# An encoder trunk in split fp32: when the reductions load their residual rows, and how the turns between stages are built

## The chip, the cores and the metric

The kernel runs on one core of one Trainium2 chip. The metric is the device time of one execution in microseconds (us), as the median of several runs; lower is better. The five engines run their own instruction streams in order: PE (TensorE, matrix products), DVE (VectorE), ACT (ScalarE), POOL (GpSimd) and SP (SyncE). In this kernel SP and POOL issue the DMAs, SP on the queue that the profile calls q1 and POOL on q0.

## What is computed

Two layers on a sequence of 1024 rows of 1024 floats. The even layer mixes with latent attention and a 2-D Fourier transform, the odd one with a spatial gating unit; each layer then has a SwiGLU block. Cut to what matters here:

```python
for layer in range(DEPTH):                       # 2
    y = even_mixer(x, ...) if layer % 2 == 0 else odd_mixer(x, ...)
    x = layer_norm(DN_ALPHA * x + y, mix_ln_g[layer], mix_ln_b[layer])
    x = layer_norm(DN_ALPHA * x + swiglu(x, ...), ffn_ln_g[layer], ffn_ln_b[layer])

def swiglu(x, w_gate, w_up, w_down):
    return (silu(x @ w_gate) * (x @ w_up)) @ w_down
```

So four times a matrix product with a wide inner dimension is followed by a sum with the residual rows x (times alpha) and a layer norm.

## The kernel before

Every product is made in split fp32: an operand is cast to a high part (ACT, line 135, names ending in h) and its remainder is formed as a low part (DVE, line 136, names ending in l). `mm3` (lines 141 to 143) then issues three matrix products per tile: high by high, low by high, high by low. The large products use Strassen's scheme in Winograd's form, seven block products of sums and differences of quarters instead of eight of the quarters.

The stages follow each other: the even mixer (0 to 566 us), `reduce` of its output, the first SwiGLU block, `reduce`, the spatial gating unit (`v_pair` and what follows), `reduce`, the second SwiGLU block, `reduce`.

`reduce` contracts a wide inner dimension (mix, ffn0, odd, ffn1 are its four calls). The inner dimension is cut into pages that earlier stages stored in memory, plain ones and sums of them (arrays named SA, SB, TA, TB). It runs the seven block products in the order p = 1, 5, 6, 4, 7, 2 and last 3, each over groups g of two pages. For each group `load` calls `stream`: SP loads the pages into tiles `rx` (pieces of 256 KB), ACT and DVE split them (tile `xoh`, `xol`), and PE multiplies them for four slots s. The call `load` runs a little ahead of the products. The residual rows are eight tiles `xt[half, s]` of 512 KB each, loaded by POOL in `residual` (line 450). Where the rows need the gain and offset of the layer norm before them, `gained` (lines 456 and 457, DVE) multiplies and adds. `add` (lines 444 and 446, DVE) adds a finished product, `norm` (lines 462 to 471) normalises, and `turn1`, `turn0` transpose the rows on PE into PSUM banks (line 363), take them back with gain and offset on ACT (line 365, one instruction per 128x128 block) and split them as operands of the next stage.

The slots of half 0 are turned at the start of the next stage, where `ffn` or `v_pair` calls the four closures in `turns`; `sums` (line 131 with splits) then forms the differences S2, S3, S4 of the turned operands. In `ffn` the unit u0 (`seven`) makes two products from the operands that are ready, u1 two more, and then the remaining ones of both. The weights of a unit are made into operands by `right_operands`: t4 and t1, b11 and b21, t2 and t3, b22. `behind` and `marks` tell the scheduler what a new instruction has to stand after; `marks[2]` is the low split of the latest load of the stream. The tiles x, q and y of `xt` are buffers which a store of the stage before may still be reading.

The order in which the instructions of each engine stand is the scheduler's, from the order of the code and these marks. On an engine nothing passes an instruction that waits.

## Time and profile before

| what | value |
|---|---|
| median of 3 runs | 2571.9 us (2570.29 to 2572.54) |
| the profiled execution, time and span | 2572.24 us, 2570.4 us |
| PE busy | 2471.8 us, 96% |
| DVE busy | 1840.0 us, 72% |
| ACT busy | 1073.5 us, 42% |
| POOL busy | 308.4 us, 12% |
| moved by DMA | 431.95 MB, mean 168 GB/s |

The span is the time from the first to the last instruction; the execution's own time is 1.8 us longer. Busy time of an engine is the time in which at least one of its instructions ran. PE's granted clock is given per stretch as a share: 1.00 is 2.4 GHz, 0.50 is 1.2 GHz. Times in the rows are us from the start of the span. In a timeline a bracket behind a row gives the time that the engine stood idle before it and what released it.

### The profile page before, as it was taken

To read this page: it belongs to the slowest core of one execution; us is meant where nothing else is said; L and a number is where in the kernel's file an instruction comes from. 1 tells how busy PE (TensorE), PEld (TensorE's weight loads), DVE (VectorE), ACT (ScalarE), POOL (GpSimd) and SP (SyncE) were. 2 spreads that over 40 slices of the span, in tenths; PEclk is the share of its full clock that TensorE was granted. 3 is DMA by queue.
4 is the path that set the end of the run, shared out by engine and by line. 5 is a ranking of instruction groups with operands and counts; after the bars stand their busy time and mean duration, and the time that the engine had idled before them with its cause. 6 is when DMAs were issued, how large, how long until landed. Compare 5 with 4: busy or idle time off the path is not lost. (4 is left out here: it accounts for less than half of the span.)

```text
span 2570.4 us, 33123 instructions
## 1 busy us (share of the span) xinstructions
PE 2471.8 (96%) x12294; PEld 2083.3 (81%) x12294; DVE 1840.0 (72%) x2673; ACT 1073.5 (42%) x1643; POOL 308.4 (12%) x511
## 2 busy tenths in 40 slices
PE   8989999999999999999999999898999999999997
PEld 6778888887778888878889997776878888887886
DVE  4448878757886667668677767788788766766757
ACT  3335545544653333334355442232474333333332
POOL 1000111010110111110011223221010101101001
PEclk9999999999999999999999999899999999999999
DMA  4122433147334454486645644457634544549554
GB/s 173 42 88 70 143 110 112 62 162 265 127 139 139 173 188 150 161 300 233 205 164 189 214 160 148 147 205 270 228 121 148 175 153 165 188 143 332 198 187 147
DMA packets 164073, 431.95 MB, mean 168 GB/s; under 512 B 19880, under 2 KB 26696, under 8 KB 163912
## 3 DMA queue, kind: packets, MB, share of 16 engines
q1 hardware_dynamic: 108216, 232.11, 27.5%
q0 software_dynamic: 55696, 197.73, 20.6%
q8 instruction: 96, 1.57, 0.3%
q14 instruction: 65, 0.53, 0.1%
HBM read 286.64 MB, written 138.41 MB: 165 GB/s over the span
## 5 line engine op out<-in xcount | busy, mean ns | idle before, releaser
L141 PE MATMUL b<-xoh,whi 128*128 128x512 f32 x1040 | 411.5, 396 | 20.3 <-ACT whi L135 18.4
L136 DVE TENSOR_TENSOR wlo<-raw,whi 128x1024 fp32r<-128x1024 f32 (+3 forms) x277 | 302.7, 1099 | 173.5 <-ACT whi L135 171.0
L135 ACT CAST whi<-raw 128x1024 fp32r<-128x1024 f32 (+3 forms) x277 | 260.6, 953 | 385.3 <-PE b L142 223.6
L135 ACT CAST xoh<-rx 128x1024 fp32r<-128x1024 f32 (+1 forms) x252 | 244.3, 1011 | 421.1 <-PE b L142 323.4
L143 PE MATMUL b<-xoh,wlo 128*128 128x512 f32 x1040 | 408.2, 393 | 0.3
L142 PE MATMUL b<-xol,whi 128*128 128x512 f32 x1040 | 408.3, 393 | 0.0
L136 DVE TENSOR_TENSOR xol<-rx,xoh 128x1024 fp32r<-128x1024 f32 (+1 forms) x252 | 287.3, 1168 | 166.1 <-ACT xoh L135 165.6
L142 PE MATMUL b<-xol,xoh 128*128 128x512 f32 x960 | 380.0, 396 | 17.7 <-DVE xol L136 17.7
L141 PE MATMUL b<-xoh 128*128 128x512 f32 x960 | 377.9, 396 | 14.5 <-ACT xoh L135 14.5
L143 PE MATMUL b<-xoh,xol 128*128 128x512 f32 x960 | 376.9, 393 | 0.0
L141 PEld LDWEIGHTS b<-xoh,whi 128*128 128x128 f32 x1040 | 197.7, 190 | 62.5 <-ACT whi L135 19.4
L143 PEld LDWEIGHTS b<-xoh,wlo 128*128 128x128 f32 x1040 | 197.1, 190 | 44.0 <-DVE wlo L136 3.1
L142 PEld LDWEIGHTS b<-xol,xoh 128*128 128x128 f32 x960 | 183.4, 191 | 59.1 <-DVE xol L136 21.0
L142 PEld LDWEIGHTS b<-xol,whi 128*128 128x128 f32 x1040 | 197.7, 190 | 41.0 <-issue 0.2
L141 PEld LDWEIGHTS b<-xoh 128*128 128x128 f32 x960 | 183.9, 192 | 54.2 <-ACT xoh L135 15.8
L143 PEld LDWEIGHTS b<-xoh,xol 128*128 128x128 f32 x960 | 183.0, 191 | 38.1
L624 ACT COPY y<-b 128x512 f32<-128x512 f32 x200 | 116.6, 587 | 214.2 <-PE b L143 210.1
L141 PE MATMUL b<-xah,whi 128*128 128x512 f32 x416 | 164.9, 396 | 0.1
L142 PE MATMUL b<-xal,whi 128*128 128x512 f32 x416 | 164.0, 394 | 0.0
L143 PE MATMUL b<-xah,wlo 128*128 128x512 f32 x416 | 162.4, 391 | 0.0
L131 DVE TENSOR_TENSOR raw<-raw,raw 128x512 f32<-128x512 f32 (+1 forms) x172 | 127.2, 739 | 24.0 <-DMA raw<-w_up 18.8
L669 DVE TENSOR_TENSOR y<-b,y 128x512 f32<-128x512 f32 x84 | 58.0, 690 | 81.4 <-PE b L143 81.4
(377 smaller groups left out, 4582.8 us busy)
## 6 DMA issues: line engine op xcount, KB each, us to landing
raw<-w_gate SPq DMA_DIRECT2D x44, 512.0 KB, 3.6
raw<-w_up SPq DMA_DIRECT2D x44, 512.0 KB
q<-w_down POOLq DMA_DIRECT2D x44, 512.0 KB, 5.2
h<-x POOLq DMA_DIRECT2D x44, 512.0 KB, 3.8
rx<-h SPq DMA_DIRECT2D x60, 256.0 KB, 3.1
rx<-w_down SPq DMA_DIRECT2D x60, 256.0 KB, 4.9
raw<-o_v SPq DMA_DIRECT2D x16, 512.0 KB, 5.2
x<-o_out POOLq DMA_DIRECT2D x16, 512.0 KB, 6.2
```

Of the source, the lines that this page charges most:

```text
L131: self.nc.vector.tensor_tensor(out, a, b, op=ALU.subtract)
L135: a = self.nc.scalar.copy(hi, src)
L136: return a.ins, self.nc.vector.tensor_tensor(lo, src, hi.bitcast(F32), op=ALU.subtract).ins
L141: mm(ps, lh, rh, start=start, stop=False, skip_group_check=skip)
L142: mm(ps, lh, rl, start=False, stop=False, skip_group_check=skip)
L143: mm(ps, ll, rh, start=False, stop=stop, skip_group_check=skip)
L624: nc.scalar.copy(t, ps)
L669: self.last_v = nc.vector.tensor_tensor(sb, ps, sb, op=op).ins
```

## The change

Four edits come together:

- `residual` takes one slot. Ahead of each load DVE writes one column of the tile (a memset of 128x1) that stands behind the low split of the latest load of the stream, and POOL's load comes after this memset. The loads of half 0 stand at groups 1 and 2 of product 1, those of half 1 in product 1's last group and product 5's first. Before, four loads stood together at group 1 of product 1 and four at group 0 of product 5.
- The first additions (product 1 into half 0) stand in group 1 of product 5 and not in the last group of product 1; the multiplications by gain and offset are spread one group later.
- `early_operands` makes the second unit's operands in two steps: t4 and t1 in the reduction, and the others behind `sums`.
- `turn0` takes two slots at once: 16 transposes into four banks, then 8 ACT instructions of 128x256 where there were 16 of 128x128, and one split of 128x1024 per operand. `ffn` turns two slots, runs two products of u0, turns the other two, and runs two of u1.

```diff
-        def residual(half):
-            for s in range(4):
-                nc.gpsimd.dma_start(xt[half, s], resid[token(half, s)])
+        def residual(half, s):
+
+            with self.behind(self.marks[2]):
+                nc.vector.memset(xt[half, s][:, 0:1], 0.0)
+            nc.gpsimd.dma_start(xt[half, s], resid[token(half, s)])
...
-                    residual(0)
                     last = self.job(st, M - 1, True) if st is self.stage["mix"] else None
-                if p == 5 and g == 0:
-                    residual(1)
+                if p == 1 and 0 < g < 3:
+                    for s in (2 * g - 2, 2 * g - 1):
+                        residual(0, s)
+                if (p == 1 and g == n - 1) or (p == 5 and g == 0):
+                    for s in (0, 1) if p == 1 else (2, 3):
+                        residual(1, s)
...
-                if p in (1, 5) and g > 1:
-                    spread([lambda s=s: gained(p == 5, s) for s in slots], g - 2, n - 2)
+                if p == 1 and g > 1:
+                    spread([lambda s=s: gained(0, s) for s in slots], g - 2, n - 1)
+                if p == 5 and g == 0:
+                    spread([lambda s=s: gained(0, s) for s in slots], n - 2, n - 1)
+                if p == 5 and g > 0:
+                    spread([lambda s=s: gained(1, s) for s in slots], g - 1, n - 1)
+                if (p, g) == (5, 1):
+                    for s in slots:
+                        add(0, s, lo, 1, True)
...
                     if g == n - 1:
-                        if p == 1:
-                            add(0, s, lo, p, True)
-                        elif p == 5:
+                        if p == 5:
...
+        def turn0(q):
+            ws = self.turned_two([xt[0, 2 * q + i] for i in range(2)], [self.m_tile("xq"[q]) for _ in range(2)], gT, bT)
+            for o, w in zip((self.A11, self.A12), ws):
+                self.late = self.split(*(x[:, q] for x in self.left(o)), w)[1]
+            for i in range(2):
+                kept[0, 2 * q + i] = tuple(w[:, :, i * P:(i + 1) * P] for w in ws)
...
+    def turned_two(self, zs, tiles, gT, bT):
+
+        nc = self.nc
+        ws = [t.rearrange("p (k c) -> p k c", k=4) for t in tiles]
+        pss = [self.bank(i, (P, 2, 256)) for i in range(4)]
+        for k in range(8):
+            for i, z in enumerate(zs):
+                nc.tensor.transpose(pss[k // 2][:, k % 2, i * P:(i + 1) * P], z[:, k * P:(k + 1) * P], self.ident)
+        for k in range(8):
+            nc.scalar.activation(ws[k // 4][:, k % 4, :], pss[k // 2][:, k % 2, :], AF.Identity, bias=bT[:, k:k + 1], scale=gT[:, k:k + 1])
+        return ws
...
+    def early_operands(self, w1, w2):
...
+        self.sub(v[:, hi], u[:, lo], g[:, lo])
+        self.sub(v[:, lo], u[:, hi], v[:, hi])
+        self.sub(v[:, lo], v[:, lo], g[:, hi])
+        cells(v, "t4", "t1")
+        yield out
+        cells(g, "b11", "b21")
+        self.sub(v[:, lo], u[:, hi], v[:, hi])
+        self.sub(v[:, hi], u[:, hi], u[:, lo])
+        cells(v, "t2", "t3")
+        cells(u[:, hi], "b22")
+        yield
...
-        u0 = unit(0, w0, "yq")
+        w1, rest = w1
+        u0, u1 = unit(0, w0, "yq"), unit(1, w1, "yq")
         turns[0]()
-        self.go(u0, 1)
+        self.go(u0, 2)
         turns[1]()
-        turns[2]()
-        self.go(u0, 1)
-        turns[3]()
-        u1 = unit(1, w1, "yq")
         self.go(u1, 2)
         sums()
+        next(rest)
         self.go(u0, 5)
...
-                if pend is not None and (n, b) in ((4, 0), (4, 1), (5, 0), (5, 1)):
-                    pend[0][(n - 4) * 2 + b]()
+                if pend is not None and b == 0 and n in (4, 5):
+                    pend[0][n - 4]()
```

What the change does to the order on the engines is shown at three places. In all rows the number behind L is the line in the kernel that the rows are of.

DVE in the reduction of ffn0, in product 1, before. L456 and L457 are the gain and offset on residual rows (`gb`), the tile x_9778 is the fourth one loaded, and the splits L136 of rx_9902 and rx_9907 are the operands of product 1's group 4.

```order
L316 TENSOR_TENSOR x_9759<-x_9573,x_9738 128x512
L317 TENSOR_TENSOR x_9758<-x_9573 128x512
L318 TENSOR_TENSOR x_9758<-x_9759,x_9573 128x512
L456 TENSOR_TENSOR q_9779<-q_9779,gb_9808 128x1024
L319 TENSOR_TENSOR x_9759<-x_9738,x_9758 128x512
L457 TENSOR_TENSOR q_9779<-q_9779,gb_9810 128x1024
L456 TENSOR_TENSOR x_9778<-x_9778,gb_9808 128x1024
L136 TENSOR_TENSOR xol<-rx_9902,xoh 128x1024
L457 TENSOR_TENSOR x_9778<-x_9778,gb_9810 128x1024
L136 TENSOR_TENSOR xol<-rx_9907,xoh 128x1024
```

The same place after. L464 is the memset, L471 and L472 are gain and offset; rx_9889 and rx_9894 are group 4, rx_9925 and rx_9930 group 5; x_9763 is the tile that was x_9778.

```order
L319 TENSOR_TENSOR x_9743<-x_9744,x_9558 128x512
L464 MEMSET x_9763 128x1
L136 TENSOR_TENSOR xol<-rx_9889,xoh 128x1024
L320 TENSOR_TENSOR x_9744<-x_9723,x_9743 128x512
L136 TENSOR_TENSOR xol<-rx_9894,xoh 128x1024
L471 TENSOR_TENSOR q_9764<-q_9764,gb_9793 128x1024
L472 TENSOR_TENSOR q_9764<-q_9764,gb_9795 128x1024
L136 TENSOR_TENSOR xol<-rx_9925,xoh 128x1024
L471 TENSOR_TENSOR x_9763<-x_9763,gb_9793 128x1024
L136 TENSOR_TENSOR xol<-rx_9930,xoh 128x1024
L472 TENSOR_TENSOR x_9763<-x_9763,gb_9795 128x1024
```

The multiplication of this tile stood ahead of both splits of group 4, and now stands between the two of group 5. Its load stood on POOL ahead of the stores ffn0SA and ffn0SB of the last page pair and now stands behind them.

POOL in the reduction of the odd mixer, before. L450 are residual loads, L814 stores a page (tp) which the stream loads again, L347 and L348 store sums of pages.

```order
L814 DMA tp_150<-x_14483 128x1024
L347 DMA oddSA_159<-raw_14829 128x1024
L348 DMA oddSB_167<-raw_14830 128x1024
L450 DMA x_14862<-xs_2_99 128x1024
L450 DMA x_14863<-xs_3_100 128x1024
L814 DMA tp_151<-x_14673 128x1024
L450 DMA q_14867<-xs_1_98 128x1024
L450 DMA q_14868<-xs_4_101 128x1024
L814 DMA tp_152<-x_14674 128x1024
```

The same place after, where L861 is the store of a page and L465 the residual load.

```order
L861 DMA tp_150<-x_14452 128x1024
L348 DMA oddSA_159<-raw_14798 128x1024
L349 DMA oddSB_167<-raw_14799 128x1024
L861 DMA tp_151<-x_14642 128x1024
L465 DMA x_14835<-xs_0_97 128x1024
L465 DMA y_14838<-xs_5_102 128x1024
L465 DMA q_14836<-xs_1_98 128x1024
L861 DMA tp_152<-x_14643 128x1024
L465 DMA q_14837<-xs_4_101 128x1024
```

The store of page tp_151 stood behind two residual loads and now stands ahead of all of them; tp_152 stands behind three.

ACT at the start of the first SwiGLU block, before. L365 takes a transposed block back from PSUM, whi_5994 is the high part of the second unit's t4 and t1.

```order
L365 ACTIVATE x_6664<-b_6665,bT_5615,gT_5614 128x128 x4
L365 ACTIVATE x_6664<-b_6666,bT_5615,gT_5614 128x128 x4
L135 CAST xah_6624<-x_6664 128x4x128 x2
L135 CAST whi_5996<-raw_5989 128x1024
L365 ACTIVATE q_6687<-b_6688,bT_5615,gT_5614 128x128
L624 COPY y_6662<-b_6649 128x512
L365 ACTIVATE q_6687<-b_6688,bT_5615,gT_5614 128x128 x3
L365 ACTIVATE q_6687<-b_6689,bT_5615,gT_5614 128x128 x4
L135 CAST xah_6624<-q_6687 128x4x128
L135 CAST whi_5994<-raw_5993 128x1024
```

The same place after, where L378 is the instruction for two slots; and, behind it, the place in the reduction of mix where the cast of t4 and t1 (now whi_6005) stands after.

```order
L378 ACTIVATE x_6622<-b_6625,bT_5615,gT_5614 128x256 x2
L378 ACTIVATE x_6622<-b_6626,bT_5615,gT_5614 128x256 x2
L135 CAST xah_6619<-x_6621 128x1024
L135 CAST xah_6619<-x_6622 128x1024
L135 CAST whi_6783<-raw_5997 128x1024
L378 ACTIVATE q_6684<-b_6686,bT_5615,gT_5614 128x256 x2
L378 ACTIVATE q_6684<-b_6687,bT_5615,gT_5614 128x256
L673 COPY y_6668<-b_6655 128x512
```

```order
L135 CAST xoh<-rx_6114 128x1024
L135 CAST xoh<-rx_6143 128x1024
L135 CAST whi_6005<-raw_6001 128x1024
L135 CAST xoh<-rx_6148 128x1024
L135 CAST xoh<-rx_6177 128x1024
```

The cast of t4 and t1 has left the turn for the reduction, and 16 instructions of 128x128 for a pair of slots have become 8 of 128x256.

## Rows read from the trace of the kernel before

**Rows 1.** PE's waits over the span: who waited for whom, total us, times, longest.

```profile
PE b L141 <- ACT whi L135: 18.4, 5, 6.0
PE b L142 <- DVE xol L136: 17.7, 8, 5.4
PE b L141 <- ACT xoh L135: 14.5, 3, 7.0
...
PE b L862 <- DVE y L873: 2.9, 2, 2.1
```

**Rows 2.** Busy us by engine (count), granted clock, DMA share, GB/s, by stretch.

```profile
1135.00:1160.00 25.00, 19.61 (x81) 15.81 (x80) 20.41 (x23) 6.40 (x7) 3.62 (x7) 0.93 1.02 385
1363.00:1400.00 37.00, 32.57 (x247) 31.72 (x247) 36.82 (x64) 20.91 (x33) 11.23 (x21) 0.93 0.66 226
```

**Rows 3.** The same view, two stretches behind PE's first stop in mix's reduction.

```profile
571.80:578.50 6.70, 6.16 (x14) 4.49 (x15) 2.41 (x2) 1.12 (x2) 0.00 (x0) 0.51 1.04 400
578.50:585.00 6.50, 6.50 (x30) 5.34 (x29) 5.50 (x8) 4.13 (x4) 0.00 (x0) 0.98 0.90 332
```

**Rows 4.** Timelines of POOL, PE and SP, reduction of mix: start, us, engine, line.

```profile
558.69 1.05 POOL L450 DMA_DIRECT2D q<-x  x2 [8.41 <-PE mm L143]
...
571.78 0.72 PE L141 MATMUL b<-xoh 128*128 128x512 f32 x1 [2.37 <-ACT xoh L135]
...
588.09 0.54 POOL L340 DMA_DIRECT2D mixSB<-raw  x1 [1.20 <-DVE raw L319]
...
594.09 0.32 SPq L383 DMA_DIRECT2D rx<-mixSB  x1
...
598.12 0.80 PE L141 MATMUL b<-xoh 128*128 128x512 f32 x1 [5.14 <-ACT xoh L135]
```

**Rows 5.** Timelines of ACT and PE, start of the first SwiGLU block.

```profile
705.87 1.20 ACT L135 CAST whi<-raw 128x1024 fp32r<-128x1024 f32 x1
...
707.12 0.80 PE L141 MATMUL b<-xoh,whi 128*128 128x512 f32 x1 [5.00 <-ACT whi L135]
...
724.09 0.62 ACT L135 CAST xoh<-q 128x512 fp32r<-128x512 f32 x1 [1.45 <-DVE q L131]
...
727.13 0.50 PE L141 MATMUL b<-xoh,whi 128*128 128x512 f32 x1 [0.97 <-ACT q L624]
```

**Rows 6.** Groups of ACT's instructions, 695 to 730: busy us, mean ns, idle before.

```profile
L365 ACT ACTIVATE q<-b,bT,gT 128x128 f32<-128x128 f32 x16 | 6.3, 609 | 0.0
...
L624 ACT COPY y<-b 128x512 f32<-128x512 f32 x4 | 2.5, 646 | 0.0
```

**Rows 7.** Timelines of POOL, DVE and PE, reductions of ffn0 and ffn1.

```profile
1139.61 0.53 POOL L450 DMA_DIRECT2D x<-xs  x1
...
1144.51 1.22 DVE L456 TENSOR_TENSOR x<-x,gb 128x1024 f32<-128x1024 f32 x1 [4.59 <-DMA x<-xs]
...
1149.20 0.80 PE L142 MATMUL b<-xol,xoh 128*128 128x512 f32 x1 [5.39 <-DVE xol L136]
...
2361.15 0.79 PE L142 MATMUL b<-xol,xoh 128*128 128x512 f32 x1 [4.94 <-DVE xol L136]
```

**Rows 8.** DMA issues, 1139.6 to 1140: KB each, us from issue to landing.

```profile
x<-xs POOLq DMA_DIRECT2D x1, 512.0 KB, 9.4
```

**Rows 9.** Timelines of POOL, ACT and PE, reduction of the odd mixer.

```profile
1743.62 0.53 POOL L450 DMA_DIRECT2D x<-xs  x1 [6.05 <-DMA tp<-x]
1744.15 0.54 POOL L814 DMA_DIRECT2D tp<-x  x1
...
1758.01 0.79 PE L141 MATMUL b<-xoh 128*128 128x512 f32 x1 [7.02 <-ACT xoh L135]
...
1770.12 0.80 PE L142 MATMUL b<-xol,xoh 128*128 128x512 f32 x1 [3.05 <-DVE xol L136]
```

**Rows 10.** DMA issues, 1744.1 to 1744.6: KB each, us to landing.

```profile
tp<-x POOLq DMA_DIRECT2D x1, 512.0 KB, 7.9
```

**Rows 11.** One line's instructions: DVE's smallest form, ns min, median, max, first and last start.

```profile
L205 DVE TENSOR_SCALAR rs<-mv x32: 135/146/155, 659.0 to 2561.2; 128x1 f32<-128x1 f32 x32
```

More of the change, by code (lines that the diff above doesn't have):

```diff
@@ L488, in turn1 @@
             kept[1, s] = l, h
-        def turn0(s):
-            l, h = self.turned(xt[0, s], (0, 1) if s % 2 == 0 else (2, 3), self.m_tile("xxqq"[s]), gT, bT)
-            self.split(*self.operand(self.A11, s), l)
-            self.late = self.split(*self.operand(self.A12, s), h)[1]
-            kept[0, s] = l, h
+        def turn0(q):
[4 more added lines that the diff above has]
+                kept[0, 2 * q + i] = tuple(w[:, :, i * P:(i + 1) * P] for w in ws)
         def sums(s):
@@ L579, in all_sums @@
                     sums(s)
-        return [lambda s=s: turn0(s) for s in slots], all_sums
+        return [lambda q=q: turn0(q) for q in range(2)], all_sums
     def bcast(self, t, src):
```

15 lines of the change are left out of this document (13 added, 2 removed).

## The prediction

> **What bounds the kernel now.** The table first: PE is busy for 96% of the span, so nothing that DVE, ACT or a queue saves counts unless PE stands still for it. PE's waits over the whole span come next [rows 1]. Three causes make up most of it: the high split of weights (18.4 us), the low split of stream operands (17.7 us) and their high split (14.5 us), 50.6 us together, plus 2.9 us for a DVE subtraction of the spatial unit. They come in a few long stops, 5 to 7 us at most, and not in many short ones. The timelines then say where the stops are: in the reduction of mix 2.37 and 5.14 us [rows 4], at the start of the first SwiGLU block 5.00 and 0.97 us [rows 5], in the reductions of ffn0 and ffn1 5.39 and 4.94 us [rows 7], in the reduction of the odd mixer 7.02 and 3.05 us [rows 9]. The second SwiGLU block starts like the first.
>
> A stop costs more than its length. Behind the first one in mix, PE ran 14 matmuls in 6.7 us with a granted clock of 0.51 (1.2 GHz), and after that 30 in 6.5 us at 0.98 (2.4 GHz) [rows 3]. At the later pace of 0.217 us the 14 would take 3.0 us. So that stop cost another 3.6 us. For other stops I take half of it, 1.8 us, between 0 and 3.6.
>
> **The change part by part.** I go by places, since in a reduction two of the four edits act together.
>
> *Reduction of mix.* Before, POOL issues its eight residual loads from 558.69 on [rows 4], the moment the stream is starved: over 571.8 to 578.5 the DMA engines are full, share 1.04 at 400 GB/s [rows 3], and PE waits for an operand until 571.78. After, no residual load is issued before the low split of the latest stream load has run, so the 2.37 us go and with them the 3.6 us of slow clock, 6.0 us. PE is then ready for the second stop at 593.0 - 6.0 = 587.0 (its start of 598.12 less 5.14 is 593.0). That stop is a store followed by its own load: POOL issues mixSB at 588.09, SP may load it at 594.09, when it has landed, and PE starts 4.0 us later [rows 4]. In the new order the eight residual loads, 4.2 MB, stand ahead of that store on POOL's queue. If they start at about 567 and have between all and half of the 400 GB/s, they take 10.5 to 21 us, and are done between 578 and 588; the store can then land between 585 (when its sums, formed late in product 1, are ready) and 592, and PE starts at 589 to 596 instead of 598.1. The gain of the whole place is 2 to 9 us; I take 5.5, the middle.
>
> The Trainium skill speaks against this edit: "DMA: Bandwidth & Descriptors", section "Rules for kernel authors", advises to issue a DMA early, compute, and wait for its semaphore late, so that the fixed cost is overlapped. By that rule the residual rows, needed only at the first additions, stood well where they were, and the edit gains nothing here; rows 3 speak the other way, since what is early there takes bytes from something that is needed sooner.
>
> *Reductions of ffn0 and ffn1.* The stop at 1149.20 ends with the low split of group 4. DVE had stood for 4.59 us in front of it, at a multiplication by the gain whose residual tile landed at 1144.5 [rows 7]. The order of the change puts both splits of group 4 ahead of any multiplication. This removes 5.39 and 4.94 us and 1.8 us each for the clock, 13.9 us together. Next late is the same tile's multiplication, now between the splits of group 5. Its load stands behind two stores and not ahead of them, like the load that POOL issues at 1139.61 and that lands 9.4 us later [rows 8], at 1149.0. Without the stop PE wants group 5 at 1149.2 - 5.4 + 5.3 (24 matmuls at 0.22) = 1149.1. Split and multiplication take 1.22 us each, so if the tile lands at 1149.0, group 5's second split ends at 1151.4, and PE stops for up to 2.3 us, plus up to 1.8 us for the clock; with one residual load less ahead of it, it lands earlier and the stop goes. I subtract 1.5 us per reduction: 11 us for both, between 6 and 14.
>
> *Reduction of the odd mixer.* POOL stands for 6.05 us in front of a residual load until 1743.62, since an old store still reads the tile. Behind it waits the store of page tp, issued at 1744.15 [rows 9] and landed 7.9 us later [rows 10], at 1752.1; PE starts 5.9 us after that, at 1758.01. In the new order this store has no residual load ahead of it. If it is issued 2 us earlier and moves without the two loads (1 MB, 2.6 us at 400 GB/s), it lands 4.6 us earlier. The second stop, 3.05 us before 1770.12, comes from a split behind the first additions, which wait for the end of product 1; these now stand a group later, and the stop goes with 1.8 us of clock. Together 9.5 us, and up to 14 if all of both stops goes. Against it: a memset or a multiplication that waits for a late tile can take the additions' place, as in the other reductions; at worst nothing is gained. I take 7.5, between 0 and 14.
>
> *Starts of the two SwiGLU blocks.* PE waits until 707.12 for the high split of the second unit's t4 and t1, which ACT makes at 705.87 [rows 5]; the change makes it in the reduction. The 5.00 us stop and the slow clock behind it (1.8 to 3.6 us) go, so PE does the four products without a break and is through at 726.2 - 5.0 - 2.7 = 718.5, where it stopped at 726.2 before. But the fifth needs operands of `sums`, and that chain runs on ACT and DVE: ACT still casts for it at 724.09, and the low part on DVE comes after that. What makes the chain start earlier is the turning by twos: 16 instructions of 128x128 took 6.3 us, 0.39 each, and a copy of 128x512 takes 0.62 (4 in 2.5 us) [rows 6]; a third of the way between them, 128x256 takes about 0.47 and 8 take 3.8. That is 2.5 us of ACT per pair and 5.0 per turn at most. From this the chain's end moves from 725.4 (724.09 + 0.62 + 0.69 of DVE) to some 722, between 720.5 and 725.4. PE then waits from 718.5, a stop of 2 to 7 us at a new place with slow clock behind it, and resumes 2 to 6.6 us before 727.13, of which the clock takes up to 2.7 us. The net is -1 to 6.6 us per block. I take 1.5 each, 3 us, nearer to the lower end, because DVE's part of the chain is no shorter.
>
> *Start of the spatial unit.* DVE is busy 36.82 of 37 us there [rows 2], and PE waits 2.9 us for its subtractions [rows 1]. DVE's work is the same, but its chain may start as much earlier as ACT finishes the turns, up to 2.5 us per pair, and a low split of weights stands earlier in its order. I take 3 us, between 0 and 7 (the 2.9, the short stops beside it, and a clock of 0.93 over 37 us, worth 2.6).
>
> *What is added.* 32 memsets of one column; DVE's smallest form in this trace takes 0.146 us [rows 11], so 4.7 us, 1.2 per reduction. DVE is busy 20.41 of 25 us in such a stretch [rows 2], and the memsets lie in its idle time: 0, and 4.7 us if all of them fall in front of a split that PE waits for. PE's transposes are as many as before.
>
> The sum is 5.5 + 11 + 7.5 + 3 + 3 = 30 us. From the profiled execution, 2572.2 us, that leaves 2542.2; it stands 0.3 us above the median, so I forecast 2542 us.
>
> **The rivals.** *Slower: DVE waits for the later residual rows.* On DVE nothing passes an instruction that waits. The loads of half 1 are now tied to splits in the last group of product 1 and the first of product 5, and their multiplications begin in group 1 of product 5. Two groups of PE are 10.6 us; a load took 9.4 us [rows 8]. If a load takes longer than these two groups, each multiplication stands in front of a split of the stream. One such stop is worth 5.4 + 1.8 = 7.2 us (what rows 7 show for the same wait); two in each of the three reductions with gain are 43 us, against the 30 gained: 2572 + 13 = 2585 us. For it: 9.4 is near to 10.6, and the DMA engines are full there (share 1.02 [rows 2]). Against: half of the loads are gone from the stretch just before.
>
> *Same: the bytes only move.* In 1135 to 1160 the DMA engines are at their limit, 385 GB/s [rows 2]. If it is the sum of stream and residual bytes that sets the pace of products 1 and 5, what one group gains the next loses, and only the two starts bring something: about 2569 us, between 2565 and 2573. The Trainium skill's rule on early issue ("DMA: Bandwidth & Descriptors", "Rules for kernel authors") would give the same. Against it: the stops end with single late pieces, and between them PE does not wait.
>
> *Half: the chains of store and load stay.* The stores of mixSB and tp remain late behind residual loads on POOL's queue, the starts of the blocks swap one stop for another with nothing left. Then mix gives 2, odd 3, ffn 9, the spatial unit 0: 2558 us.
>
> *More: all stops named go.* These are 2.4 + 5.1 + 2 x 6 + 5.4 + 4.9 + 7.0 + 3.1 + 2.9 = 42.8 us, and some 1.8 us or more for each of nine; about 60 us, 2512 us.
>
> **How the numbers follow.** My forecast has a chance of 0.45, and covers 2530 to 2553. Half 0.20, more 0.11, same 0.12, slower 0.12. Some 0.2% (5 us) is what a measurement of this kernel can tell from no change. Faster by over that is 0.45 + 0.20 + 0.11 and a little of the same case, 0.78; same 0.11; slower 0.11. The range that leaves out no more than 2 in 10 goes from 2517 (most of the case of more) to 2566 (all of the half case); left out are the slower case and most of the same one.
>
> **What would show it.** Right: no stop of PE over 1 us at the places of 571.8, 707.1, 1149.2, 1770.1 and 2361.2; the load of mixSB issued before 592; tp landed before 1749; the stop of the SwiGLU starts moved to the first product that uses `sums`. Wrong: a wait of DVE at the multiplication by the gain in front of a split of product 5, a memset that waits for a store, or a stop in front of group 5 longer than 2.3 us.

## The result and the profile after

| | before | after |
|---|---|---|
| median | 2572.2 us (4 runs, 2570.3 to 2576.7) | 2552.4 us (4 runs, 2550.5 to 2552.7) |
| ratio to before | | 0.9925, interval 0.9911 to 0.9938 |
| profiled execution, time and span | 2572.24, 2570.4 us | 2552.27, 2550.5 us |
| PE busy | 2471.8 us | 2465.7 us |
| DVE busy | 1840.0 us | 1840.6 us |
| ACT busy | 1073.5 us | 1062.7 us |

The change is faster by 19.9 us, 0.75%, clear of the interval. The forecast was 2542 us, 30 us faster; the time lies in the range 2517 to 2566. A third of the gain forecast did not come. The runs below say which terms were off, and the largest error lies in one of them.

The same view as in [rows 1], PE's waits of the kernel after, has these rows (who waited for whom, total us, times, longest):

```profile
PE b L141 <- ACT xoh L135: 19.8, 6, 6.0
PE b L142 <- DVE xol L136: 13.1, 9, 3.9
PE b L141 <- ACT whi L135: 8.9, 3, 6.4
```

Half of the wait for the high split of weights is gone, and a quarter of the wait for low splits. The row of the high splits `xoh` has grown, but not by the stream: 7.9 of its 19.8 us are two stops for the operands that `sums` makes, 3.72 and 4.18 us at the starts of the SwiGLU blocks, so one wait has taken another's place there. For operands of the stream it fell from 14.5 to 11.9 us.

**Where the time went.** PE runs 12,294 matmuls and transposes in both traces. The start of the one with a given number can be compared between two traces, so the difference at the end of a stage less that at its beginning is what the stage gained. This table has it in us (negative is earlier), for the change and for all runs of this study, each against the kernel before. The stages are, by the times of before: mix 566 to 640, start of the first SwiGLU block 693 to 760, ffn0 1118 to 1260, start of the spatial unit 1345 to 1440, odd 1745 to 1800, start of the second SwiGLU block 1893 to 1945, ffn1 2330 to 2400. "Rest" is all else.

| kernel | mix | start 1 | ffn0 | spatial | odd | start 2 | ffn1 | rest | sum |
|---|---|---|---|---|---|---|---|---|---|
| forecast | -5.5 | -1.5 | -5.5 | -3.0 | -7.5 | -1.5 | -5.5 | 0 | -30.0 |
| after | -5.1 | -1.8 | -4.4 | -6.5 | +1.5 | -0.1 | -5.0 | +1.4 | -20.0 |
| e1 tie only | -3.5 | +0.3 | -2.5 | -0.3 | -3.9 | +0.2 | -4.3 | -1.6 | -15.6 |
| e2 additions only | -0.1 | +0.1 | -3.0 | -0.2 | +1.9 | +0.7 | -3.7 | -1.0 | -5.3 |
| e3 early operands only | +1.0 | +1.3 | +1.2 | -1.1 | -0.3 | +4.1 | -0.1 | -1.2 | +4.9 |
| e4 turns by twos only | +0.2 | -0.2 | -0.3 | -6.5 | -0.3 | +0.2 | +0.2 | +0.2 | -6.5 |
| e5 after, odd's places undone | -3.3 | -2.7 | -4.2 | -6.5 | -0.5 | -0.8 | -5.0 | +0.3 | -22.7 |
| e6 after, no early operands | -3.4 | -0.4 | -4.2 | -6.5 | +1.6 | +0.6 | -4.1 | -3.2 | -19.6 |
| e7 after, no memset | -0.5 | -2.9 | -2.7 | -6.2 | +2.1 | -0.4 | -5.9 | -0.9 | -17.4 |
| e8 e5 and sums by operand | -3.9 | -7.3 | -4.0 | -6.3 | -0.8 | -5.7 | -5.0 | -2.4 | -35.4 |
| e9 e8, mix later, order | -1.0 | -7.2 | -7.1 | -6.2 | -1.2 | -5.7 | -8.1 | +0.2 | -36.3 |
| e10 e8, odd's loads last | -3.5 | -7.2 | -4.0 | -6.0 | +1.1 | -5.7 | -4.9 | -1.3 | -31.5 |
| e11 e9, behind the load | -3.4 | -7.2 | -7.1 | -6.3 | -1.5 | -5.7 | -8.1 | +0.2 | -39.1 |
| e12 e8 and order | -3.6 | -7.2 | -7.1 | -6.3 | -0.8 | -5.7 | -8.1 | -3.2 | -42.0 |

"Rest" moves by 3 us and more between kernels whose code there is the same, and a stage by 1 to 2; the last section shows why. So only differences above some 2 us in one stage are read as an effect of an edit, unless the stops behind them are named.

**The places, in the profile of after.** Mix, timelines of POOL, PE and SP, as in [rows 4]:

```profile
569.13 0.54 POOL L465 DMA_DIRECT2D x<-x  x1 [4.04 <-DVE x L464]
...
580.26 0.54 POOL L341 DMA_DIRECT2D mixSB<-raw  x1 [0.66 <-DVE raw L320]
...
590.28 0.50 PE L141 MATMUL b<-xoh 128*128 128x512 f32 x1 [3.78 <-ACT xoh L135]
...
593.39 0.32 SPq L396 DMA_DIRECT2D rx<-mixSB  x1
...
599.85 0.50 PE L141 MATMUL b<-xoh 128*128 128x512 f32 x1 [1.14 <-ACT xoh L135]
```

The residual loads wait for the memset and start at 569.13, where seven of the eight started from 558.69 on and one at 549.75. The first stop of [rows 4] is gone. The store of mixSB is issued 7.8 us earlier than before and its load only 0.7 us earlier, so it landed 12.5 us after its issue and not 6.0. The DMA issues from 580.2 to 580.7 (KB, us to landing) say so:

```profile
mixSB<-raw POOLq DMA_DIRECT2D x1, 512.0 KB, 12.5
```

The reduction of ffn0, timelines of DVE and PE, as in [rows 7]:

```profile
1141.87 1.23 DVE L471 TENSOR_TENSOR x<-x,gb 128x1024 f32<-128x1024 f32 x1 [5.06 <-DMA x<-xs]
1143.01 1.22 DVE L136 TENSOR_TENSOR xol<-rx,xoh 128x1024 fp32r<-128x1024 f32 x1
...
1144.28 0.50 PE L142 MATMUL b<-xol,xoh 128*128 128x512 f32 x1 [1.18 <-DVE xol L136]
...
1153.60 0.50 PE L142 MATMUL b<-xol,xoh 128*128 128x512 f32 x1 [0.86 <-DVE xol L136]
```

DVE still stands for 5 us in front of the same late tile, but now between the splits of group 5, and PE pays 1.18 us for it where it paid 5.39, with no slow clock behind it.

The reduction of the odd mixer, timelines of POOL, PE and DVE, as in [rows 9]:

```profile
1723.65 0.60 POOL L861 DMA_DIRECT2D tp<-x  x1 [5.18 <-DVE wlo L846]
...
1738.41 0.79 PE L141 MATMUL b<-xoh 128*128 128x512 f32 x1 [6.01 <-ACT xoh L135]
...
1759.68 1.19 PE L141 MATMUL b<-xoh 128*128 128x512 f32 x4 [0.96 <-ACT xoh L135]
...
1762.97 2.37 DVE L471 TENSOR_TENSOR x<-x,gb 128x1024 f32<-128x1024 f32 x2
1765.24 2.36 DVE L472 TENSOR_TENSOR x<-x,gb 128x1024 f32<-128x1024 f32 x2
1767.52 1.29 DVE L457 SCALAR_TENSOR_TENSOR x<-x,b 128x512 f32<-128x512 f32 x2
...
1772.30 6.91 DVE L136 TENSOR_TENSOR xol<-rx,xoh 128x1024 fp32r<-128x1024 f32 x6
...
1774.72 0.50 PE L142 MATMUL b<-xol,xoh 128*128 128x512 f32 x1 [3.86 <-DVE xol L136]
```

The store of tp took 6.5 us to land, by the DMA issues from 1723.6 to 1724:

```profile
tp<-x POOLq DMA_DIRECT2D x1, 512.0 KB, 6.5
```

The first stop is 6.01 us where it was 7.02. The second one (3.05 us at the end of product 1) is gone, and two new ones stand in product 5 and at the start of product 6: the last multiplications and eight additions stand ahead of the split that PE waits for. The view by stretch (PE, PEld, DVE, ACT, POOL busy, clock, DMA share, GB/s) shows DVE without a pause from 1750 to 1774:

```profile
1738.00:1750.00 12.00, 11.59 (x39) 9.34 (x40) 11.61 (x13) 4.27 (x5) 2.63 (x5) 0.73 0.75 260
1750.00:1762.00 12.00, 11.04 (x49) 8.84 (x48) 12.00 (x14) 4.11 (x4) 0.00 (x0) 1.00 0.76 272
1762.00:1774.00 12.00, 8.86 (x40) 7.00 (x38) 12.00 (x15) 4.00 (x4) 0.00 (x0) 1.00 0.29 92
```

The starts of the two SwiGLU blocks, PE's stops, as in [rows 5]:

```profile
718.24 1.89 PE L141 MATMUL b<-xoh,whi 128*128 128x512 f32 x3 [3.72 <-ACT xoh L135]
...
1919.46 1.89 PE L141 MATMUL b<-xoh,whi 128*128 128x512 f32 x3 [4.18 <-ACT xoh L135]
```

The stop for the weights' split is gone and stands in front of the first product that uses `sums`, as forecast.

### The profile page after: what moved, and what is told of

It is laid out like the page before. It is cut to its first block, busy times and chain, and to the rows that moved or that the text cites. A ratio compares the mean times of both kernels' runs of the same rounds, so it can differ in the third digit from the quotient of the medians.

```text
span 2550.5 us, 33081 instructions
## 1 busy us (share of the span) xinstructions
PE 2465.7 (97%) x12294; PEld 2077.1 (81%) x12294; DVE 1840.6 (72%) x2695; ACT 1062.7 (42%) x1583; POOL 309.5 (12%) x511
## 4 chain that ended last, share of the span: by engine, by line
PE 76%; DVE 9%; issue 6%; DMA 4%; ACT 3%; SPq 1%; POOL 1%; DVEq 0%; ACTq 0%; POOLq 0%
PE b L142 17%; PE b L143 17%; PE b L141 17%; PE S L1313 6%; PE b L909 5%; PE mm L141 4%; PE mm L142 4%; PE mm L143 4%; PE mm L1332 2%; DVE xol L136 2%; DMA rx<-h 1%; ACT xoh L135 1%; DVE raw L131 1%; SPq L396 0%; DMA oddSA<-raw 0%
## 5 line engine op out<-in xcount | busy, mean ns | idle before, releaser
L136 DVE TENSOR_TENSOR wlo<-raw,whi 128x1024 fp32r<-128x1024 f32 (+3 forms) x277 | 302.4, 1099 | 163.3 <-ACT whi L135 161.9
L136 DVE TENSOR_TENSOR xol<-rx,xoh 128x1024 fp32r<-128x1024 f32 (+1 forms) x252 | 287.7, 1168 | 141.2 <-ACT xoh L135 130.6
L141 PE MATMUL b<-xoh 128*128 128x512 f32 x960 | 373.6, 394 | 11.9 <-ACT xoh L135 11.9
```

The costliest lines, as they stand in the source:

```text
L136: return a.ins, self.nc.vector.tensor_tensor(lo, src, hi.bitcast(F32), op=ALU.subtract).ins
L141: mm(ps, lh, rh, start=start, stop=False, skip_group_check=skip)
```

## The experiments

Each kernel was run beside the kernel before on the same chip. The median of the kernel before was 2568.6 to 2572.2 us in the five groups of runs (after; e1 to e4; e5 to e8; e9 and e10; e11 and e12), so across groups the ratios are compared. The numbers by stage are those of the table above, each from one trace.

**e1, the tie alone.** In the kernel before, `residual` and the places of its calls as in the change, all else as before.

```diff
-        def residual(half):
-            for s in range(4):
-                nc.gpsimd.dma_start(xt[half, s], resid[token(half, s)])
+        def residual(half, s):
+            with self.behind(self.marks[2]):
+                nc.vector.memset(xt[half, s][:, 0:1], 0.0)
+            nc.gpsimd.dma_start(xt[half, s], resid[token(half, s)])
...
+                if p == 1 and 0 < g < 3:
+                    for s in (2 * g - 2, 2 * g - 1):
+                        residual(0, s)
```

> The kernel before with one edit: residual loads one slot at a time behind a memset, in the new places; multiplications, first additions, operands and turns as before. Theory (the tie lets the stream's loads go first, the shift of the multiplications is what removes the stops in the reductions of ffn0 and ffn1): mix gains about 5 us, the odd reduction 0 to 4, ffn0 and ffn1 lose or gain under 2 each, since the multiplication of a late tile still stands ahead of group 4's splits and its tile lands later; in total 2563 to 2568. Rival (the tie alone makes the gain of all reductions): 2554 to 2558. Rival (the bytes only move): 2570 to 2574.

Measured: 2556.5 us (2553.6 to 2556.9), ratio 0.9938 (0.9923 to 0.9952), inside the range of the first rival. The loads in their new places and tied bring most of the whole change alone, though some 3 of its trace's 15.6 us are clock (see the last section). What the new places bring in the kernel before without the tie was not run; e7 has that with the other edits. My theory is wrong on ffn0 and ffn1: they gain 2.5 and 4.3 us without any shift of the multiplications in the code. The tie changes DVE's order too. These rows are the two splits of group 4 and the multiplication of the late tile in ffn0:

```profile
1136.55 2.35 DVE L136 TENSOR_TENSOR xol<-rx,xoh 128x1024 fp32r<-128x1024 f32 x2
...
1144.97 1.23 DVE L458 TENSOR_TENSOR x<-x,gb 128x1024 f32<-128x1024 f32 x1 [2.53 <-DMA x<-xs]
```

The multiplication now stands behind both splits, as in the change, and PE stops at group 5, for 2.66 us where it was 5.39.

**e2, the shift of multiplications and additions alone.** In the kernel before, `gained` one group later and the first additions at product 5's second group.

```diff
+                if p == 5 and g > 0:
+                    spread([lambda s=s: gained(1, s) for s in slots], g - 1, n - 1)
+                if (p, g) == (5, 1):
+                    for s in slots:
+                        add(0, s, lo, 1, True)
```

> The kernel before with one edit: multiplications one group later and the first additions in product 5's second group; residual loads as before. Theory: the stops of 5.4 and 4.9 us in ffn0 and ffn1 go (about 6 us each), the second stop of the odd reduction goes (4.5) and product 5 there loses as much or more again because DVE gets 7 us more work in 4 groups, mix is unchanged within 1 us; in total 2558 to 2564. Rival (the shift does nothing without the tie): 2570 to 2574.

Measured: 2567.6 us (2563.7 to 2570.6), ratio 0.9985 (0.9976 to 0.9994), in neither range: the theory gave ffn0 and ffn1 6 us each. The shift too is worth 3.0 and 3.7 us in ffn0 and ffn1, so each of the two edits removes about half of the same stop or more, and together they bring 4.4 and 5.0, not the sum. The odd reduction loses 1.9 us, as expected: its second stop is gone, and this one, PE's at the start of product 6, has come:

```profile
1789.25 0.79 PE L142 MATMUL b<-xol,xoh 128*128 128x512 f32 x1 [5.19 <-DVE xol L136]
```

The residual loads are those of before there, so the shift makes this stop, not the tie.

**e3, the two-step operands alone.** In the kernel before, `early_operands` and `next(rest)` behind `sums`, turns by single slots.

```diff
-                    w0[l].append(self.right_operands(*gate_up(l)(1)))
+                    rest = self.early_operands(*gate_up(l)(1))
+                    w0[l].append((next(rest), rest))
...
         sums()
+        next(rest)
         self.go(u0, 5)
```

> The kernel before with one edit: t4 and t1 of the second unit split in the reduction, the rest behind the sums; turns by single slots. Theory: the 5 us stop ahead of the second unit goes in both blocks, and PE stops instead in front of the first product that needs the sums, which still start as late; gain 0 to 2 us per block, 2568 to 2572. Rival (the stop simply goes): 6.5 us per block, 2559.

Measured: 2576.6 us (2573.2 to 2582.8), ratio 1.0023 (1.0009 to 1.0036): slower, which neither theory gave. The starts of the blocks lose 1.3 and 4.1 us. PE's stops at the second block show why; the first is a wait for the high part of A11 or A12, the other for ACT's copy of the accumulator into which the first product from the sums adds:

```profile
1924.42 1.31 PE L141 MATMUL b<-xah,whi 128*128 128x512 f32 x2 [2.76 <-ACT xah L135]
...
1938.34 0.80 PE L141 MATMUL b<-xoh,whi 128*128 128x512 f32 x1 [5.48 <-ACT q L650]
```

With the weights ready PE is at the turned operands before ACT has turned them 128 columns at a time. One stop of 4.85 us and one of 0.97 became two, 8.2 us together.

**e4, the turns by twos alone.** In the kernel before, `turned_two` and `turn0(q)`, with `ffn` and `v_pair` calling two closures.

```diff
-                if pend is not None and (n, b) in ((4, 0), (4, 1), (5, 0), (5, 1)):
-                    pend[0][(n - 4) * 2 + b]()
+                if pend is not None and b == 0 and n in (4, 5):
+                    pend[0][n - 4]()
```

> The kernel before with one edit: turns of half 0 by two slots, 8 instructions of 128x256 on ACT for 16 of 128x128. Theory: the spatial unit's start gains about 6.6 us as in the changed kernel, since DVE's chain starts earlier; the two SwiGLU starts gain 0 to 3 each because the weights' split comes earlier on ACT as well; 2559 to 2566. Rival (ACT was never last, DVE's work sets it): within 1 us of before, 2571 to 2573.

Measured: 2565.0 us (2562.6 to 2567.0), ratio 0.9976 (0.9967 to 0.9986). The spatial unit's start gains 6.5 us, the same as in the whole change, and PE's stops of 2.9 and 1.3 us there have shrunk to this one:

```profile
1390.43 0.39 PE L873 MATMUL b<-wlo,xah 128*128 128x256 f32 x1 [0.58 <-DVE wlo L136]
```

At the starts of the SwiGLU blocks it brings nothing (0.2 us) while the weights' split is late.

**e5, the change with the shift undone in the odd reduction.**

```diff
+        shift = not left
...
+                if not shift and p in (1, 5) and g > 1:
+                    spread([lambda s=s: gained(p == 5, s) for s in slots], g - 2, n - 2)
...
+                        if p == 1 and not shift:
+                            add(0, s, lo, p, True)
```

> The changed kernel with one part undone in the odd reduction alone: multiplications and first additions where they stood before (the residual loads stay tied). Theory (in the odd reduction's product 5, four groups long, DVE has no room for two more multiplications and four more additions, and PE pays at the start of product 6): the odd reduction ends about 5 us earlier against the changed kernel, the stops of 0.96 and 3.86 us in product 5 and 6 are gone and the one of 3.05 us at the end of product 1 is back; 2546 to 2548. Rival (the late residual loads themselves cost it): unchanged at 2551 to 2553.

Measured: 2546.4 us (2545.1 to 2549.5), ratio 0.9906 (0.9891 to 0.9921). The stops came as the theory has them: those of products 5 and 6 are gone, and the one at the end of product 1 is back. (Its row names a memset that ran on DVE just before; a split on DVE ends there as well.)

```profile
1738.57 0.79 PE L141 MATMUL b<-xoh 128*128 128x512 f32 x1 [6.09 <-ACT xoh L135]
...
1751.00 0.53 PE L142 MATMUL b<-xol,xoh 128*128 128x512 f32 x1 [3.05 <-DVE x L465]
```

But the odd reduction is only 2.0 us better than in the change (-0.5 against +1.5), not 5. The sign is sure: the kernels with the shift there have +1.5 to +2.1 (after, e2, e6, e7), those with the additions in their old place -0.3 to -3.9. That the total fits the theory's range is luck. The profiled execution, 2549.5 us, was 3 us above e5's median, and where the other 4 us between the medians of e5 and the change come from, no trace shows.

**e6, the change without the two-step operands.**

```diff
-                    rest = self.early_operands(*gate_up(l)(1))
-                    w0[l].append((next(rest), rest))
+                    w0[l].append(self.right_operands(*gate_up(l)(1)))
```

> The changed kernel without the two-step operands: the second unit's weights are all made at one place as before. Theory (with turns by twos the early t4 and t1 let PE get to the sums sooner but the sums are no earlier, so the edit is worth little): first block 1 to 2 us later, second block within 1 us, so 2552 to 2555. Rival (the edit costs time by itself, as it did alone with 5.5 us): 2547 to 2549.

Measured: 2553.4 us (2551.7 to 2555.0), ratio 0.9931 (0.9916 to 0.9946). The first block is 1.4 us later than in the change, the second 0.7. With turns by twos the edit no longer costs anything and is worth 1 us a block, at the limit of what can be told here.

**e7, the change without the memsets.**

```diff
-            with self.behind(self.marks[2]):
-                nc.vector.memset(xt[half, s][:, 0:1], 0.0)
             nc.gpsimd.dma_start(xt[half, s], resid[token(half, s)])
```

> The changed kernel without the memsets: the residual loads stand in the new places of the code but are tied to nothing. Theory (it is the tie that keeps the residual rows out of the stream's way): in mix the loads are issued at about 559 again and the stop of 2.4 us with its slow clock is back, 3 to 6 us, in the ffn reductions 0 to 2 each; 2556 to 2563. Rival (the new places alone do it): within 1.5 us of the changed kernel, 2551 to 2554.

Measured: 2554.7 us (2554.5 to 2557.6), ratio 0.9940 (0.9923 to 0.9956), 1.3 us below the range of the theory and 0.7 above the rival's. Its interval overlaps that of the change, so the tie's worth in the total, some 2 us, is not clear of the noise; by stages, it is in mix. There the loads are issued from 562.74 on, and the gain falls from 5.1 to 0.5 us; ffn0 loses 1.7, and ffn1 is no worse. But the stop that comes back in mix is not the first one. These rows are POOL, ACT and PE there:

```profile
562.74 0.53 POOL L463 DMA_DIRECT2D x<-x  x1
...
573.85 1.05 ACT L135 CAST xoh<-rx 128x1024 fp32r<-128x1024 f32 x1 [2.83 <-DMA rx<-mixTA]
577.68 1.05 ACT L135 CAST xoh<-rx 128x1024 fp32r<-128x1024 f32 x1 [2.77 <-DMA rx<-mixSB]
...
576.22 0.50 PE L142 MATMUL b<-xol,xoh 128*128 128x512 f32 x1 [0.59 <-DVE xol L136]
...
596.91 0.80 PE L141 MATMUL b<-xoh 128*128 128x512 f32 x1 [7.56 <-ACT xoh L135]
```

The two loads of q (issued from 563.27 on, before from 558.69) stand 4.6 us later even without the tie, and PE's first stop is gone. But the stream's next pages then come 3.8 us apart (569.97 to 585.42 for five casts on ACT), where in the change four came within 5.4 us (570.48 to 575.85). DVE forms the sums behind these splits, so the store of mixSB is issued at 585.91 and not at 580.26.

**e8, sums operand by operand.** As e5, and in `all_sums` S2 of all four slots comes first, then S4, then S3.

```diff
-                for s in slots:
-                    sums(s)
+                for i in range(3):
+                    for s in slots:
+                        sums(s, i)
```

> As the run with the odd reduction's places undone, and the sums made operand by operand (S2 of all slots, then S4, then S3) and not slot by slot. Theory (PE's stop at the SwiGLU starts, 3.7 and 4.2 us, is the wait for the first operand that is whole in all slots): S2 is whole after a third of DVE's chain, the stop goes, 3 to 6 us per block, and 2536 to 2542 in all. Rival (DVE's whole chain sets the end of these products whatever its order): the stop moves to a later product, within 2 us of that run, 2545 to 2548.

Measured: 2536.1 us (2532.3 to 2536.9), ratio 0.9861 (0.9846 to 0.9876). The starts gain 7.3 and 5.7 us against before, where e5 had 2.7 and 0.8. Of PE's stop of 4.2 us at the second block 1.00 us is left, and of the 3.7 us at the first this:

```profile
715.96 0.49 PE L142 MATMUL b<-xol,whi 128*128 128x512 f32 x1 [0.65 <-DVE xol L136]
```

A product reads one operand of all four slots. Slot by slot the first operand is whole only when nearly all of the chain has run.

**e9, two more edits on e8.** In mix the residual loads of half 1 at product 5's second group, behind the stores on POOL; in ffn0 and ffn1 multiplications and additions of half 0 in the order of the loads.

```diff
+                if last is not None and (p, g) == (5, 1):
+                    for s in slots:
+                        residual(1, s)
...
-                    spread([lambda s=s: gained(0, s) for s in slots], g - 2, n - 1)
+                    spread([lambda s=s: gained(0, s) for s in (1, 2, 3, 0)], g - 2, n - 1)
```

> As the run with sums operand by operand, with two more edits: in mix the residual loads of half 1 come behind the stores of the last page sums on POOL's queue (product 5, group 1), and in ffn0 and ffn1 the multiplications of half 0 and their additions go in the order of the loads, the slot loaded last at the end. Theory: in mix the store of mixSB lands 7 to 8 us earlier, since four loads of 512 KB less are ahead of it, and the stop of 4.2 us and what follows it go, 3 to 6 us; in ffn0 and ffn1 the stops of 1.6 and 0.85 us at groups 5 of product 1 go, 2 to 3 us each; 2524 to 2530. Rival (the stop in mix is set by the stream's own loads, the late tile by something else): 2534 to 2538.

Measured: 2535.4 us (2534.7 to 2536.5), ratio 0.9868 (0.9851 to 0.9884), outside the theory's range and inside the rival's, and no better than e8. The order does what the theory says: ffn0 and ffn1 gain 3.1 us more each, and their stops are gone. In mix the store of mixSB is indeed early, its load is issued at 586.47 and not at 592 or 593. Yet PE's stop has become longer, and mix keeps only 1.0 us. ACT and PE show the wait:

```profile
594.70 2.94 ACT L135 CAST xoh<-rx 128x1024 fp32r<-128x1024 f32 x3 [8.55 <-DMA rx<-mixSB]
...
595.79 0.80 PE L141 MATMUL b<-xoh 128*128 128x512 f32 x1 [10.16 <-ACT xoh L135]
```

The load that follows the store took 8.2 us, beside four residual loads issued from 579.36 to 581; ACT stood at its cast with two other casts behind it.

**e10, the odd reduction's loads last.** As e8, with half 0 loaded behind the splits of product 1's last group and its multiplications and first additions in product 5.

```diff
+                if not shift and (p, g) in ((1, n - 1), (5, 0)):
+                    for s in slots:
+                        residual(0 if p == 1 else 1, s)
```

> As the run with sums operand by operand, but in the odd reduction the loads of half 0 stand behind the splits of product 1's last group, those of half 1 at product 5's first, and all multiplications of half 0 and the first additions in product 5. Theory (the page's load, 256 KB, takes 7 us there because residual loads issued in the same 6 us share the DMA engines with it): the stop of 6.2 us at the last group of product 1 falls to 3 to 4 us; DVE gets more work in product 5, and PE stops there for more than the 4.8 us of the changed kernel, so the reduction as a whole loses; 2538 to 2546. Rival (the load is late because its store is late, whatever else is in flight): the stop stays at 5.5 to 6.5 us.

Measured: 2540.3 us (2536.6 to 2544.0), ratio 0.9887 (0.9870 to 0.9903). PE's stop falls from 6.2 to 3.5 us. From the landing of the store of tp to PE's start it takes 6.6 us (1726.03 to 1732.63), in e8 8.3 (1725.11 to 1733.42); this 1.7 us is what the theory of loads in flight beside the page's load has. The other 0.9 us come from the store, which lands earlier against PE's place in the program, so the rival has a part too. Product 5 pays more:

```profile
1732.63 0.50 PE L141 MATMUL b<-xoh 128*128 128x512 f32 x1 [3.53 <-ACT xoh L135]
...
1754.57 0.97 PE L141 MATMUL b<-xoh 128*128 128x512 f32 x3 [2.12 <-ACT xoh L135]
...
1770.78 0.79 PE L142 MATMUL b<-xol,xoh 128*128 128x512 f32 x1 [5.02 <-DVE xol L136]
```

**e11, mix's later loads one group on.** As e9, with half 1 at product 5's last group and its first additions in product 6.

```diff
-                if last is not None and (p, g) == (5, 1):
+                if last is not None and (p, g) == (5, n - 1):
```

> As the run with mix's later loads and the order of the multiplications, but in mix the loads of half 1 stand behind the low split of product 5's last group, so behind the stream's own load of mixSB and not beside it, and their first additions in product 6's second group. Theory (a load that waits for a store is as late through what is in flight beside it as through what is ahead of the store): the load of mixSB lands 3 to 5 us after its issue and not 8.2, PE's stop of 10.2 us falls to 4 to 7, mix gains 4 to 7 us against the kernel before; 2526 to 2532. Rival (what is in flight beside it does not matter): the load still takes 7 to 9 us, and 2534 to 2537.

Measured: 2531.6 us (2530.8 to 2533.1), ratio 0.9848 (0.9834 to 0.9862). The total is in the expected range, but the edit did not do what it was for: the mark is the split of the group's second operand, and the late page is in the first. POOL and SP show it:

```profile
584.72 2.19 POOL L466 DMA_DIRECT2D x<-x  x4 [4.72 <-DVE x L465]
...
586.46 0.32 SPq L396 DMA_DIRECT2D rx<-mixSB  x1
```

The four loads were still issued ahead of the load of mixSB. It took 6.7 us and PE stopped for 8.3. That the stop would go if nothing were beside this load is not shown.

**e12, e8 with the order of the loads only**, mix as in the change.

> As the run with sums operand by operand and one edit: multiplications and first additions of half 0 in ffn0 and ffn1 in the order of the loads; mix as in the changed kernel. Theory: ffn0 and ffn1 gain 3 us each more, mix is as in the changed kernel, 4 to 5 us better than before; 2528 to 2532. Rival (run to run differences in mix hide it): 2533 to 2537.

Measured: 2530.8 us (2528.7 to 2534.0), ratio 0.9845 (0.9830 to 0.9860). It is 39 us faster than before, by the ratios some 21 us faster than the change, and the same as e11 within the measurement.

## Why the prediction came out as it did

**Odd reduction: forecast -7.5, measured +1.5, and outside its bounds of 0 to -14.** This one term is 9 of the 10 us that were missing. The other errors nearly cancel: 3.5 us too little was forecast for the spatial unit, and 4.5 too much for the rest together. Two steps failed in the odd reduction.

The step "these now stand a group later, and the stop goes" was right on the stop and left out what the moved work meets. The shift brings two pairs of multiplication and addition by gain and offset, 2.4 us each, and four additions of a product, 0.6 each, some 7 us of DVE's work, into product 5. In the odd reduction a product has four groups, about 21 us of PE, and DVE's splits, multiplications and additions there filled it already. The prediction named a memset or a multiplication that waits for a late tile as the risk; but in the rows of after DVE does not wait there, it is simply full (12.00 of 12 us, twice). e2 shows the same stop with the loads of before, and e5 without the shift does not have it. The exchange is one stop of 3.05 us for two of 4.8 together, and costs 2.0 us by e5.

The step on the store of tp was right on the store and wrong on what follows it. It landed 3.3 us earlier, counted from PE's place in the program (1730.12 with the 18.6 us already gained, against 1752.06); 4.6 was forecast. But I let PE start 5.9 us after that, as before, and it took 8.3. The residual loads had left their place ahead of the store and now were in flight beside the load of the same page. e10 takes most of them away and has 6.6 us, with the stop at 3.5.

**Mix: forecast -5.5, measured -5.1.** The first stop went, 2.4 us and its slow clock, and PE reached its second 6.5 us earlier (586.5 against 593.0). From there the working failed, and the number is near by luck. The store landed at 592.8 where 592 was the late end, and from then to what hangs on it PE took 7.0 us (599.85) where I counted 4.0 as before, so it came later than the 589 to 596 forecast. But from 590.28 PE ran 19 matmuls of the group on other pages, which I had not thought of. e7 shows that the tie is what brings mix's gain: without it mix gains 0.5, with it and the loads as in the change 3.3 to 5.1 in seven kernels. The prediction puts the second stop down to the loads ahead of the store; e9 and e11 show that this is not all. In e9 the store landed at 586.46, in e8 at 592.13, but its load then took 8.2 us where it took 5.2 in e8: what is moved from ahead of the store falls beside the load.

The prediction drew from the Trainium skill's rule to issue a DMA early ("DMA: Bandwidth & Descriptors", "Rules for kernel authors") that this edit would gain nothing. That did not come: e1 loads the residual rows later, and is 15 us faster. The rule speaks of overlap with compute, which e1 keeps, so this tells against my use of it more than against the rule.

**ffn0 and ffn1: forecast -5.5 each, measured -4.4 and -5.0.** The order of DVE, the new place of the wait and its size came as worked out: a stop of up to 2.3 us was forecast for a tile that lands too late for group 5, and 1.18 us came in ffn0 and 1.67 in ffn1, with 0.86 a group later in both. What the text did not see is that two edits make this order: by e1 and e2 the tie and the shift each take the late multiplication from in front of group 4, and each brings 2.5 to 4.3 us alone. e9 and e12 remove what was left by multiplying in the order of the loads.

**Starts of the SwiGLU blocks: forecast -1.5 each, measured -1.8 and -0.1.** The mechanism was right: the stop moved to the first product that uses `sums`, at 3.7 and 4.2 us. I said that DVE's part of the chain is no shorter; e8 shows that its order was what counted.

**Start of the spatial unit: forecast -3, measured -6.5.** A size was off, in a term whose range went to 7. I counted ACT's time saved by pairs and stayed low, while 0.58 us is left of the stops of 2.9 and 1.3, and the granted clock over 37 us, 0.93 in [rows 2], is 1.00 (first row below), with DVE as busy as before. e4 gives it to the turns by twos alone. By [rows 6] I had estimated 3.8 us for eight instructions of 128x256, and they took 3.76 (second row):

```profile
1353.00:1390.00 37.00, 36.15 (x297) 35.55 (x296) 36.79 (x63) 20.04 (x32) 11.23 (x21) 1.00 0.70 244
...
690.32 3.76 ACT L378 ACTIVATE x<-b,bT,gT 128x256 f32<-128x256 f32 x8 [3.62 <-PE b L376]
```

**What was added: 0, and it cost nothing that can be seen.** A memset took 59 ns, under the 146 of the row that bounded it. But four memsets in ffn0 and ffn1 waited for a DMA, three of them for the store of a page, 0.8 to 1.9 us each and 5.7 us together; the second row is one of them:

```profile
L464 DVE MEMSET x<- x20: 59/59/59, 568.8 to 2350.7; 128x1 f32 x20
...
2325.86 0.06 DVE L464 MEMSET q<- 128x1 f32 x1 [1.79 <-DMA ffn1TB<-q]
```

The prediction named a memset that waits for a store as a sign of being wrong. The sign came and meant nothing here: PE has no stop over 0.5 us in these reductions before the one at group 5.

**The rivals.** The slower one, DVE standing at the later residual rows in product 5, did not come: the waits of multiplications in after (5.06, 5.36 and 2.28 us) lie in product 1. Its place was right, though: product 5 of the odd reduction is where time was lost, through full and not through waiting. "The bytes only move" fell with e1, which moves the same bytes and gains 15 us. The measured time is 0.6 us inside what the forecast covers (2530 to 2553), and "half", 2558, is nearer to it than 2542. Its reason, that the chains of store and load stay, is in part what came; but of its parts only ffn came (9, measured 9.4), while mix (2) measured 5.1, odd (3) -1.5 and the spatial unit (0) 6.5, so that its sum is near is luck. Of the signs of being right one failed: the load of mixSB was issued at 593.39, not before 592.

## What to carry to other kernels

Work that is moved out of a stop needs a place: add up what the engine already does in the stretch where it lands, for the shortest loop that runs through the same code, before the stop is counted as gained. Tying a transfer that is not urgent to the split of the data that is kept some 3 us in mix that the new places alone did not; but then each chain of a store and its load has to be followed to the end, since what is moved from ahead of the store may end up beside the load. Where several parts together make one operand, make one operand whole before the next is begun: this cost no instruction and was worth 10 us here.

## What the runs showed of the hardware that was not expected

The slow clock behind a stop does not come each time. The kernels before, after and e5 have the same code and, within 0.1 us, the same stop of 2.2 us at the same place of the spatial unit; these are the 7 us behind it, of the kernel after and of e5 (clock is the third number from the end, the mean over the 7 us of the levels 1.00 and 0.50):

```profile
1547.50:1554.50 7.00, 6.63 (x32) 5.29 (x32) 6.87 (x14) 1.14 (x2) 1.80 (x3) 1.00 0.65 246
...
1546.00:1553.00 7.00, 7.00 (x27) 5.48 (x27) 6.83 (x14) 1.15 (x2) 1.46 (x2) 0.76 0.57 221
```

In the first the clock stayed at 1.00, and PE did 32 matmuls; in the second it was 0.76, and PE did 27. The kernel before had 0.76 there too. The stop of 3.05 us at the end of product 1 in the odd reduction has it as well. These are 7 us behind it in e1 and in e5:

```profile
1760.00:1767.00 7.00, 6.94 (x30) 5.74 (x31) 7.00 (x10) 1.06 (x1) 1.05 (x2) 1.00 0.88 313
...
1751.00:1758.00 7.00, 7.00 (x24) 5.59 (x25) 7.00 (x7) 0.74 (x1) 1.05 (x2) 0.76 0.93 319
```

So e1's 3.9 us in the odd reduction holds some 3 us of clock, for stops (5.53 and 3.05 us) that are nearly those of e5 (6.09 and 3.05), which gained 0.5: the clock behind the first stop, too, was 0.76 in e1 and 0.56 in e5. It works the other way at the end of the program, where the kernel after and e5 lost 2.2 us against the others: 0.5 by a stop of 1.8 us for 1.27, and the rest by a clock of 0.76 behind it, where before, e6 and e7 had 1.00. A single trace's stage is then good to 1 or 2 us for each long stop in it, and which stops are there tells more of an edit than the stage's time.
